# A decoder block's attention stage: the rotary steps on GpSimd one to a slot, filler blocks dealt out evenly, and weight splitting taken off GpSimd behind attention

## The chip, the core and the metric

The kernel runs on one core of one Trainium2 chip, as one program in one launch. The metric is the time of an execution in microseconds (us) on the device; lower is better. A core has five engines with a queue of instructions each: TensorE (PE, matrix products and transposes into PSUM), VectorE (DVE), ScalarE (ACT), GpSimd (POOL) and SyncE (SP, which here only issues DMAs). They run side by side and wait for one another through semaphores. Each takes its own instructions in order, so an instruction that waits holds up everything behind it on its engine.

## What is computed

The reference is one layer of a decoder on 512 tokens of width 1024, in float32:

```python
h = rms_norm(x, norm_mix[l]);  proj = h @ w_in[l]
u, q, kc, vc, ksl, vsl, kwn, vwn, g_nsa, g_merge = jnp.split(proj, IN_SPLITS, axis=-1)
y_pool = pool_mixer(u, w_pool[l], pool_scale[l])
y_nsa = nsa_mixer(q, kc, vc, ksl, vsl, kwn, vwn, g_nsa, ...)
g_a, g_b = jnp.split(sigmoid(g_merge), 2, axis=-1)
merged = g_a * (y_pool @ w_proj_pool[l]) + g_b * (y_nsa @ w_proj_nsa[l])
x = x + merged @ w_out[l]
h = rms_norm(x, norm_mlp[l])
x = x + jnp.square(jax.nn.relu(h @ w_ff1[l])) @ w_ff2[l]
return rms_norm(x, norm_final)
```

`nsa_mixer` is attention with 16 heads of 64 dimensions and two key/value groups, in three branches: over compressed blocks, over selected blocks and over a sliding window. With 512 tokens every block is selected and the window covers everything, so the last two branches are two causal attentions with keys and values of their own. Queries and keys are turned by rotary position tables (`apply_rope`): `y = x*cos + rot(x)*sin`, where `rot` swaps the two halves of a head.

## The kernel before

**Stages.** A first stage projects keys, values, the pooling mixer, the first three query blocks (`q0` to `q2`) and the gates `ga`. The attention stage follows, then the merge with the remaining columns of `w_proj_nsa` (keys `pn2` to `pn7`) and `w_out` (keys `wo`), then the MLP, whose large products are formed from seven smaller ones each (so some sums of weight blocks are made in DRAM beforehand, by DMAs that accumulate).

**Precision.** Each float32 operand is split in a high part `h` and a rest `l`, and a product is three matmuls (h·h, h·l, l·h). Weights arrive by DMA from SP in one of four raw buffers (`emit_load`, line 235), ACT writes `h` (line 351), and the rest is a subtraction (line 353), half a weight block (128x512) at a time. `emit_prep_half` gives the second half's subtraction to GpSimd while `mode["pool"]` is set and to VectorE otherwise. It is set ahead of attention and reset only ahead of the MLP.

**Attention.** A *slot* is one head, one block of 128 queries and one or both of the two causal branches. A pair of heads has 12 slots: four short ones (query blocks 0 and 1, both branches in one slot, `half` 0) and eight long ones (query blocks 2 and 3, one branch a slot, `half` 1, 384 or 512 keys). Eight pairs make 96 slots. The loop at the end of the stage deals with one slot a turn: scores of slot i+1 on PE (line 1014), mask and minimum on DVE (line 1036, `smax`), exponential on ACT (line 1046, `expo`), normalising and gating weights of slot i-1 on GpSimd (line 1059, `weight`), transposes of slot i-4 on PE (line 1076; `LAG` is 4), their split on ACT and DVE (lines 1087 and 1091), and two slots later the products with the values (line 1110). Probabilities have five buffers (`P_BUFS`). Compressed scores of the next pair are a generator of small steps (`cmp_scores`, lines 950 to 986) that `step_side` advances once a slot; three of its steps are on GpSimd (lines 973, 975, 976).

**Fillers.** PE work that does not hang on the slots is put between them: `FILL2` lists 13 blocks, the query blocks `q3` to `q7` and the eight blocks of the other gate (`gb0` to `gb7`), each of 24 matmuls of 128x512 in four pieces of six (`pieces`, line 394, PSUM tile `psF`), followed by the first block of `w_proj_nsa` (`pn0`). `fill()` emits one piece. The loop calls it until `want` is reached, a share that grows evenly with the slots, and once more in each of the first five slots. A query block is followed by its rotary turn, and `fill2` gives back without a piece while a rotary turn of an earlier query block is under way (`while scored["rope"]`).

**Rope.** `rope` (a generator, advanced once a slot) copies the block from PSUM on ACT (`rx`, line 618), lets four DMAs on SP's queue write the swapped halves (`rs`, line 621), multiplies by the cosine table (line 626) and the sine table (line 629) in two halves of 256 columns each, on GpSimd during attention, and adds the two on DVE (line 634). Four multiplications are issued in four consecutive slots, whatever their kind. Then `q_done` splits the block into the `Q` tile (lines 659 to 664).

**Sums in DRAM.** `make_sum` copies a block of `w_ff` to DRAM from SP's queue (line 265), and `add_sum` adds another to it by an accumulating DMA that GpSimd's queue issues (line 273). In the loop, `add_sum(last)` runs in every fourth slot and stands behind that slot's weights.

The order of the instructions on each engine is fixed when the program is built; a scheduler places them by the order of the code and by its own estimate of when they are ready, and `issue_after` (`behind`) ties one instruction to a place behind another.

Of the kernel before, what the change touches and what calls it, by code (L numbers as in the profile page):

```python
# [16 lines left out]
ALU = mybir.AluOpType  # L17
# [45 lines left out]
def trunk(ctx: ExitStack, tc: tile.TileContext, A, out):  # L63
    nc = tc.nc
    PE, ACT, DVE, POOL = nc.tensor, nc.scalar, nc.vector, nc.gpsimd
    PSUM = bass.MemoryType.PSUM

    def pool(name, **kw):
        return tc.tile_pool(name=name, bufs=1, reuse_waits="tile", **kw)
# [35 lines left out]
    def add_key(k):  # L105
        i = int(k[-1]) if k[-1].isdigit() else None
        if k in IN_COLS:
            add_cols(k, w_in, IN_COLS[k])
        elif k[:2] in ("wk", "wv"):
            w = A["w_c" + k[1] + "1"][0]  # L110
            add_w(k, [(w[512 * i:512 * i + 512, :].rearrange("(k p) c -> p k c", p=128), 0)])
        elif k[0] == "V":
            k0, k1 = ((0, 3), (3, 6), (6, 8))[i]
            wv = w_in[k0 * 128:k1 * 128, :].rearrange("(k p) c -> p k c", p=128)
            add_w(k, [(wv[:, :, 1920:2048], 0), (wv[:, :, 2176:2352], 128)])
        elif k == "wpool":
            add_w(k, [(w_pool.rearrange("g c d -> c g d"), 0)])
        elif k[:2] == "pp":
            add_w(k, [(w_pp[:, 256 * i:256 * i + 256].rearrange("(k p) c -> p k c", p=128), 0)])
        else:  # L120
            c0 = {"u": 0, "q": 512, "ga": 2352, "gb": 3376}[k[:-1]]
            add_cols(k, w_in, c0 + 128 * i)
# [1 line left out]
    IN_COLS = {"ck": 1536, "cv": 1664, "ks": 1792, "kw": 2048}  # L124
    P1 = ("ck ks u0 wk0 wk1 u1 wk2 u2 kw wk3 cv V0 V1 V2 wv0 u3 wv1 q0 wv2 wpool ga0 ga1 wv3 ga2 q1 "
          "ga3 ga4 ga5 q2 ga6 ga7 pp0 pp1 pp2 pp3").split()
    FILL2 = "gb0 q3 q4 q5 gb1 gb2 q6 gb3 q7 gb4 gb5 gb6 gb7".split()
    for k in P1 + FILL2:
        add_key(k)
    for j in range(8):  # L130
# [83 lines left out]
    held, begun = {}, deque()  # L214

    def emit_load():
# [20 lines left out]
        if sums_after(i):  # L237
            make_sum(began)
        if i >= len(P1) + len(FILL2) + 4 and (len(begun) > 2 or begun and st["sums"] == len(jobs)):
            add_sum()  # L240
        return True

    def sums_after(i):

        if i < MLP0:
            return len(P1) + 3 <= i < len(P1) + len(FILL2) + 8
        return i % 3 == 0
# [10 lines left out]
    def make_sum(load):  # L258

        if st["sums"] < len(jobs):  # L260
            to, q, _ = jobs[st["sums"]]
            while any(q is jobs[n][0] for n in begun):
                add_sum()
            with tc.issue_after(load.ins):
                nc.sync.dma_start(to, q)
            begun.append(st["sums"])
            st["sums"] += 1

    def add_sum(behind=None):

        to, _, q = jobs[begun.popleft()]
        with tc.issue_after(behind.ins) if behind else nullcontext():
            POOL.dma_start(to, q, accum_op=ALU.add)  # L273

    part = {}
    mode = {"pool": False, "first": POOL}
# [105 lines left out]
    def use(key):  # L382
        i = st["use"]
        st["use"] += 1
        assert WL[i][0] == key, (WL[i][0], key)
        while st["prep"] <= i:
            emit_prep_half()
        return hls.pop(i)
# [21 lines left out]
    def step_side():  # L410
        for _ in range(len(side)):
            g = side.popleft()
            try:
                next(g)
                side.append(g)
            except StopIteration:
                pass

    def drain_side():
        while side:  # L420
            step_side()
# [57 lines left out]
    op = e2.enter_context(pool("op"))  # L479
# [49 lines left out]
    def behind(made):  # L529
        return tc.issue_after(made.ins)  # L530
# [22 lines left out]
    def evac0(i, after=None):  # L553
        sl = slice(128 * i, 128 * i + 128)
        for a in range(2):
            ks = slice(4 * a, 4 * a + 4)
            r = ACT.activation(hT[0][:, ks, sl], trs[i][a], AF.Copy)
            with behind(after) if after else nullcontext():
                v = DVE.tensor_tensor(hT[1][:, ks, sl], trs[i][a], hT[0][:, ks, sl].bitcast(F32), op=ALU.subtract)
        return r, v  # L560
# [9 lines left out]
    r, _ = evac0(1)  # L570
# [32 lines left out]
    cosT, sinT = cst[:, C_COS:C_COS + S], cst[:, C_SIN:C_SIN + S]  # L603
# [4 lines left out]

    scored = {"pairs": 0, "rope": 0}
    last_exp = []  # L610

    def rope(ps, scale, done, after=0):

        assert not scored["rope"]
        scored["rope"] = 1
        xr = ap.tile([128, S], F32, tag="rx", bufs=1, name="rx")
        sw = ap.tile([128, S], F32, tag="rs", bufs=1, name="rs")
        ACT.activation(xr, ps, AF.Copy, scale=scale)
        for b in range(4):
            a = b ^ 1  # L620
            nc.sync.dma_start(sw[32 * b:32 * b + 32, :], xr[32 * a:32 * a + 32, :])
        yield
        eng = POOL if mode["pool"] else DVE
        hs = [slice(0, S // 2), slice(S // 2, S)]
        for c in hs:
            eng.tensor_tensor(xr[:, c], xr[:, c], cosT[:, c], op=ALU.mult)
            yield
        for c in hs:
            eng.tensor_tensor(sw[:, c], sw[:, c], sinT[:, c], op=ALU.mult)
            yield  # L630
        yield
        for c in hs:
            yield
            DVE.tensor_tensor(xr[:, c], xr[:, c], sw[:, c], op=ALU.add)
        while scored["pairs"] < after:
            yield
        for _ in done(xr):
            yield
        scored["rope"] = 0
# [28 lines left out]
    with ExitStack() as c1:  # L668
# [184 lines left out]
        for k in P1[2:]:  # L853
            i = int(k[-1]) if k[-1].isdigit() else None
# [35 lines left out]
    with ExitStack() as c2:  # L890
        p2 = c2.enter_context(pool("p2"))
        ps2 = c2.enter_context(pool("ps2", space=PSUM))
        def fill2():
            for k in FILL2:
                i = int(k[-1])
                if k[0] == "q":
                    while scored["rope"]:
                        yield True
                    post = (lambda i: lambda ps: rope(ps, 1.0, q_done(i), i - 2))(i)
                else:  # L900
                    def post(ps, i=i):
                        ACT.activation(GB[:, i, :], ps, AF.Copy)
                yield from fm(k, ps2, post)
            free.append(True)
            split_ready()
            early[0] = use("pn0") + (ps2.tile([128, S], F32, tag="F", bufs=F_BANKS, name="psF"),)
            for k in range(7):
                while (k, 1) not in split:
                    yield True
                proj_k(early[0], k)  # L910
                if k % 2 or k == 6:
                    ahead()
                    yield
# [20 lines left out]
        fdone = [0]  # L934

        def fill(n=1):
            for _ in range(n):
                if next(filler, True):
                    return False
                fdone[0] += 1  # L940
            return True
# [47 lines left out]
        slots = []  # L989
# [95 lines left out]
        def turn_hi(i):  # L1085
            src, dH, dL = turn_views(i)
            ACT.activation(dH, src, AF.Copy)  # L1087
# [35 lines left out]

        side.append(cmp_scores(0))
        while 0 not in PTc:
            fill()
            step_side()
        n = len(slots)
        total = 4 * len(FILL2) + 4
        done0 = fdone[0]  # L1130
        after = deque()
        score_pe(0)
        for i in range(n + LAG + PLAG):
            if i < n:
                p = slots[i][0]
                if i % 12 == 3 and p + 1 < NPAIR:
                    while p + 1 not in Q:
                        fill()
                        step_side()
                if i % 12 == CMP_AT and p + 1 < NPAIR:  # L1140
                    side.append(cmp_scores(p + 1))
            if i + 1 < n:
                score_pe(i + 1)
                scored["pairs"] = (i + 2) // 12
            t = i - LAG
            if 0 <= t < n:
                turn_pe(t)
                turn_hi(t)
            if i < n:
                smax(i)  # L1150
                expo(i)
            if 0 <= i - 1 < n:
                last = weight(i - 1)
            if i % 4 == 3 and len(begun) > 1:
                add_sum(last)
            if 0 <= t < n:
                turn_lo(t)
            step_side()
            want = done0 + (total - done0) * (i + 1) // (n + LAG + PLAG)
            while fdone[0] < want and fill():  # L1160
                pass
            if i < 5:
                fill()
            j = t - PLAG
            if 0 <= j < n and j % 2 == 1 and pv(j):
                o_evac(*slots[j][0:2])
        for _ in filler:
            pass
        drain_side()
        early[1] = use("pn1") + (ps2.tile([128, S], F32, tag="F", bufs=F_BANKS, name="psF"),)  # L1170
        with tc.issue_after(last_exp[0].ins):
            for j in range(8):
# [93 lines left out]
    with ExitStack() as c3:  # L1266
        q3 = c3.enter_context(pool("q3"))
# [385 lines left out]
```

## Time and profile before

| | us |
|---|---|
| median of 3 runs | 813.62 (812.95 to 814.96) |
| the profiled execution, its own time | 811.65 |
| span of that execution, first to last instruction | 809.8 |
| TensorE busy in it | 788.0 (97%) |
| VectorE busy | 621.4 (77%) |
| ScalarE busy | 491.3 (61%) |
| GpSimd busy | 207.9 (26%) |

The profile is of one execution. Busy times are by engine; a matmul's end is modelled and matmuls overlap, so PE counts as busy also where it is not at its peak, and what tells is its idle time and who ended it. In the views by stretch of time each row gives busy time and number of instructions of each engine, then PEclk, the share of TensorE's clock that was granted, then the mean busy share of the DMA engines and what they moved. In the views of groups, "idle before" is idle time of that engine just ahead of the group, with the work that ended it. Attention lies between about 182 and 390 us of the span.

### The profile page before, as it was taken

The page shows a single profiled execution, that of the slowest core. Times are in us where ns is not written, and L with a number is a line of the kernel's source. Part 1 is how long each engine was busy: PE and PEld are TensorE (multiplying, and loading weights), DVE is VectorE, ACT ScalarE, POOL GpSimd, SP SyncE. Part 2 cuts the span into 40 slices and gives each one's busy share as a digit, 9 for nine tenths or more (in the row PEclk, how much of TensorE's full clock was granted, in tenths as well). Part 3 has the DMA queues.
Part 4 walks back from the last instruction along what each step waited for, and adds up shares of the span by engine and source line. Part 5 has one row for each costly group of instructions (what it writes and reads, how often), then busy time and mean ns, then how long its engine had stood idle before and what let it go on. Part 6 is the DMA issues. An engine that isn't in the chain of part 4 may idle for free.

```text
span 809.8 us, 14149 instructions
## 1 busy us (share of the span) xinstructions
PE 788.0 (97%) x5163; PEld 709.1 (88%) x5163; DVE 621.4 (77%) x1217; ACT 491.3 (61%) x968; POOL 207.9 (26%) x273
## 2 busy tenths in 40 slices
PE   8999999998999999999999999999999999999996
PEld 7889878887788888888788899999999999999996
DVE  5796744547888888888664579996899689978975
ACT  6576533327878788899434476934773477347833
POOL 4000000028777867674334100111111110000000
PEclk9999999999999999999999999999999999999999
DMA  9554632357456524554954807999899997754522
GB/s 306 141 161 120 167 92 92 104 162 164 66 134 136 129 72 93 104 132 93 313 146 155 203 2 217 317 242 284 243 285 225 286 262 207 211 165 156 185 76 105
DMA packets 128752, 136.65 MB, mean 169 GB/s; under 512 B 5349, under 2 KB 117001, under 8 KB 128522
## 3 DMA queue, kind: packets, MB, share of 16 engines
q1 hardware_dynamic: 107274, 113.98, 43.3%
q0 software_dynamic: 21120, 20.97, 18.2%
q8 instruction: 41, 0.67, 0.3%
q10 hardware_dynamic: 288, 0.79, 0.3%
q14 instruction: 29, 0.24, 0.1%
HBM read 131.01 MB, written 44.04 MB: 216 GB/s over the span
## 4 chain that ended last, share of the span: by engine, by line
PE 75%; DVE 14%; ACT 5%; issue 3%; POOL 2%; DMA 1%; SPq 0%; ACTq 0%; DVEq 0%; POOLq 0%
PE psF L394 22%; PE psB L1380 15%; PE psB L394 12%; PE psB L1499 9%; PE psO L1110 3%; PE psT L1076 3%; PE psS L1014 3%; DVE wl L308 2%; PE psV L394 2%; PE psF L451 1%; DVE w3l L308 1%; PE psC L714 1%; DVE P L1036 1%; ACT wh L306 1%; POOL P L1059 1%
## 5 line engine op out<-in xcount | busy, mean ns | idle before, releaser
L394 PE MATMUL psF<-R,wh 128*128 128x512 f32 x512 | 166.6, 404 | 0.8 <-ACT GB L688 0.6
L306 ACT ACTIVATE wh<-raw 128x1024 fp32r<-128x1024 f32 x70 | 74.0, 1058 | 74.0 <-PE psB L1499 32.6
L351 ACT ACTIVATE wh<-raw 128x512 fp32r<-128x512 f32 (+1 forms) x100 | 60.1, 620 | 82.5 <-PE psF L394 38.2
L394 PEld LDWEIGHTS psF<-R,wh 128*128 128x128 f32 x512 | 92.4, 189 | 19.0 <-ACT GB L688 0.9
L273 POOL DMA_DIRECT2D S<-w_ff x40 | 46.4, 1160 | 233.1 <-DMA S<-w_ff 163.5
L394 PE MATMUL psF<-R,wl 128*128 128x512 f32 x256 | 101.9, 398 | 0.4 <-DVE wl L353 0.4
L308 DVE TENSOR_TENSOR wl<-raw,wh 128x1024 fp32r<-128x1024 f32 x70 | 85.3, 1219 | 16.8 <-ACT wh L306 16.7
L1059 POOL TENSOR_SCALAR P<-P,sm,GT 128x128 f32<-128x128 f32 (+3 forms) x128 | 86.0, 708 | 42.2 <-DVE sm L1056 28.7
L353 DVE TENSOR_TENSOR wl<-raw,wh 128x512 fp32r<-128x512 f32 (+1 forms) x74 | 53.5, 734 | 33.3 <-ACT wh L351 32.3
L1046 ACT ACTIVATE P<-P,sm 128x128 f32<-128x128 f32 (+3 forms) x128 | 71.0, 556 | 9.5 <-DVE sm L1036 8.5
L1036 DVE CUSTOM_DVE_ANT_0 P<-psS,cst 128x128 f32<-128x128 f32 (+3 forms) x128 | 59.7, 484 | 6.8 <-PE psT L1076 5.1
L1380 PE MATMUL psB<-R,wh 128*128 128x256 f32 x352 | 64.1, 282 | 0.0
L1087 ACT ACTIVATE PT<-psT 128x512 fp32r<-128x512 f32 (+2 forms) x96 | 49.5, 520 | 19.7 <-PE psT L1076 19.0
L353 POOL TENSOR_TENSOR wl<-raw,wh 128x512 fp32r<-128x512 f32 x28 | 38.1, 1364 | 88.4 <-ACT wh L351 86.1
L306 ACT ACTIVATE w3h<-raw 128x1024 fp32r<-128x1024 f32 x35 | 37.0, 1056 | 39.2 <-PE psB L1499 17.0
L1091 DVE TENSOR_TENSOR PT<-psT,PT 128x512 fp32r<-128x512 f32 (+2 forms) x96 | 56.5, 594 | 3.4 <-ACT PT L1087 2.6
L394 PEld LDWEIGHTS psF<-R,wl 128*128 128x128 f32 x256 | 48.3, 189 | 11.4 <-DVE wl L353 0.6
L1076 PE MATMUL psT<-ident,P 128*128 128x128 f32 x320 | 51.6, 275 | 4.8 <-POOL P L1059 4.0
L1380 PEld LDWEIGHTS psB<-R,wh 128*128 128x128 f32 x352 | 54.1, 189 | 0.3 <-DVE R L1322 0.2
L308 DVE TENSOR_TENSOR w3l<-raw,w3h 128x1024 fp32r<-128x1024 f32 x35 | 42.7, 1220 | 14.4 <-ACT w3h L306 14.4
L1076 PEld LDWEIGHTS psT<-ident,P 128*128 128x128 f32 x320 | 40.0, 142 | 14.7 <-POOL P L1059 6.9
L1380 PE MATMUL psB<-R,wl 128*128 128x256 f32 x176 | 49.5, 281 | 0.0
(385 smaller groups left out, 2295.7 us busy)
## 6 DMA issues: line engine op xcount, KB each, us to landing
raw<-w_ff SPq DMA_DIRECT2D x55, 512.0 KB, 5.2
S<-w_ff POOLq DMA_DIRECT2D x40, 512.0 KB, 7.7
raw<-S SPq DMA_DIRECT2D x40, 512.0 KB, 4.4
raw<-w_in SPq DMA_DIRECT2D x32, 512.0 KB, 3.9
S<-w_ff SPq DMA_DIRECT2D x30, 512.0 KB, 5.4
S<-S SPq DMA_DIRECT2D x10, 512.0 KB, 6.2
raw<-w_proj_nsa SPq DMA_DIRECT2D x8, 512.0 KB, 4.2
raw<-w_out SPq DMA_DIRECT2D x8, 512.0 KB, 3.5
```

The costliest lines, as they stand in the source:

```text
L306: ACT.activation(h, t, AF.Copy)
L308: DVE.tensor_tensor(l, t, h.bitcast(F32), op=ALU.subtract)
L351: ACT.activation(h[:, sl], t[:, sl], AF.Copy)
L353: eng.tensor_tensor(l[:, sl], t[:, sl], h[:, sl].bitcast(F32), op=ALU.subtract)
L394: PE.matmul(ps, a, b, start=first and j == 0, stop=last and j == n - 1, skip_group_check=True)
L1036: DVE.tensor_tensor_reduce(out=P[:, o:o + n].rearrange("p (a c) -> p a c", c=128), in0=s, in1=m, scale=1.0, scalar=3e38, op0=ALU.add, op1= ...
L1046: last_exp[:] = [ACT.activation(c, c, AF.Exp, bias=sm[:, 0, e:e + 1], scale=-1.0, accum_out=sm[:, 1, e:e + 1])]
L1059: r = POOL.tensor_scalar(P[:, o:o + n], P[:, o:o + n], sm[:, 2, e:e + 1], GT[:, qb, c + e:c + e + 1], op0=ALU.mult, op1=ALU.mult)
L1076: PE.transpose(pt[:, 128 * j:128 * j + 128], P[:, 128 * j:128 * j + 128], ident)
L1091: DVE.tensor_tensor(dL, src, dH.bitcast(F32), op=ALU.subtract)
L1380: PE.matmul(out, w[u][:, k, 128 * f:128 * f + 128], XB[x][v][:, k, :], **kw)
L1499: PE.matmul(out, YB[y][u][:, k, 128 * f:128 * f + 128], w[v][:, k, :], **kw)
```

## The change

Four things are changed.

1. **Rope.** The four multiplications are taken in the order cosine and sine of the first half of the columns, then of the second, and on GpSimd each is issued only in a turn of the loop in which `slot["long"]` is set: from the fifth turn on, where the slot whose weights were just issued is a long one. Each is tied to a place behind those weights. The sum of the first half is issued as soon as the second half's cosine step is; the other one turn after the last multiplication.
2. **Fillers.** `FILL2` alternates gate and query blocks (`gb0 q3 gb1 q4 gb2 q5 gb3 q6 q7 gb4 ...`). Ahead of the loop at most eight pieces are emitted, and in a turn at most two; the extra piece in each of the first five turns is gone.
3. **Sums.** `add_sum` starts in turn 11 in place of turn 3.
4. **Weights.** `mode["pool"]` is reset at the end of the loop, so that behind attention VectorE subtracts both halves of a weight block.

```diff
-    FILL2 = "gb0 q3 q4 q5 gb1 gb2 q6 gb3 q7 gb4 gb5 gb6 gb7".split()
+    FILL2 = "gb0 q3 gb1 q4 gb2 q5 gb3 q6 q7 gb4 gb5 gb6 gb7".split()
...
+    slot = {"long": False, "scaled": None}
...
         hs = [slice(0, S // 2), slice(S // 2, S)]
         for c in hs:
-            eng.tensor_tensor(xr[:, c], xr[:, c], cosT[:, c], op=ALU.mult)
-            yield
-        for c in hs:
-            eng.tensor_tensor(sw[:, c], sw[:, c], sinT[:, c], op=ALU.mult)
-            yield
+            for t, table in ((xr, cosT), (sw, sinT)):
+                while mode["pool"] and not slot["long"]:
+                    yield
+                with behind(slot["scaled"]) if mode["pool"] else nullcontext():
+                    eng.tensor_tensor(t[:, c], t[:, c], table[:, c], op=ALU.mult)
+                yield
+                if c is hs[1] and t is xr:
+                    DVE.tensor_tensor(xr[:, hs[0]], xr[:, hs[0]], sw[:, hs[0]], op=ALU.add)
         yield
-        for c in hs:
-            yield
-            DVE.tensor_tensor(xr[:, c], xr[:, c], sw[:, c], op=ALU.add)
+        DVE.tensor_tensor(xr[:, hs[1]], xr[:, hs[1]], sw[:, hs[1]], op=ALU.add)
...
         while 0 not in PTc:
-            fill()
+            if fdone[0] < 8:
+                fill()
             step_side()
...
                 last = weight(i - 1)
-            if i % 4 == 3 and len(begun) > 1:
+                slot.update(long=i > 3 and slots[i - 1][1] == 1, scaled=last)
+            if i > 7 and i % 4 == 3 and len(begun) > 1:
                 add_sum(last)
...
             want = done0 + (total - done0) * (i + 1) // (n + LAG + PLAG)
-            while fdone[0] < want and fill():
-                pass
-            if i < 5:
-                fill()
+            for _ in range(2):
+                if fdone[0] < want:
+                    fill()
...
         drain_side()
+        mode["pool"] = False
         early[1] = use("pn1") + (ps2.tile([128, S], F32, tag="F", bufs=F_BANKS, name="psF"),)
```

## The prediction

> **What bounds the kernel now.** I read the page first, then busy time by stretch, then who made TensorE (PE) wait, then the chain of waits and the timeline where it waits most. Engines busy:
>
> ```profile
> PE 788.0 (97%) x5163; PEld 709.1 (88%) x5163; DVE 621.4 (77%) x1217; ACT 491.3 (61%) x968; POOL 207.9 (26%) x273
> ```
>
> PE sets the end, and since the change leaves its matmuls as they are, time can only come from what PE loses: idle time and a lower clock. The stretches of attention and of the stage behind it (columns: length, then PE, PEld, DVE, ACT, POOL busy, granted clock, DMA):
>
> ```profile
> 182.10:200.10 18.00, 15.21 (x85) 12.38 (x84) 13.79 (x53) 12.15 (x38) 14.25 (x20) 0.91 0.74 169
> 200.10:223.40 23.30, 21.35 (x144) 18.10 (x142) 20.01 (x66) 19.91 (x55) 16.95 (x25) 1.00 0.46 70
> 223.40:238.50 15.10, 14.53 (x79) 12.02 (x79) 12.42 (x39) 11.50 (x31) 10.19 (x15) 1.00 0.36 103
> 238.50:271.30 32.80, 32.61 (x214) 28.82 (x213) 29.00 (x100) 26.42 (x72) 24.58 (x34) 1.00 0.75 154
> 271.30:302.90 31.60, 30.53 (x198) 26.77 (x198) 28.39 (x89) 26.14 (x69) 22.66 (x33) 1.00 0.38 93
> 382.00:393.00 11.00, 9.33 (x47) 7.57 (x46) 6.42 (x10) 7.92 (x15) 2.61 (x2) 1.00 1.13 286
> 393.00:487.00 94.00, 93.82 (x468) 78.19 (x466) 59.37 (x82) 44.26 (x83) 22.66 (x17) 1.00 0.54 154
> ```
>
> Length less PE busy: idle 2.79, 1.95, 0.57, 0.19, 1.07, 1.67 and 0.18 us. The first two rows are pairs 0 and 1 of heads, and they hold more than half. The merge behind attention leaves PE no idle time to win. Who ended the waits inside attention:
>
> ```profile
> PE psT L1076 <- POOL P L1059: 4.0, 3, 2.2
> PE psB L394 <- ACT mH L1280: 1.7, 1, 1.7
> PE psT L1076 <- ACT pc L986: 0.7, 1, 0.7
> PE psT L984 <- DVE PT L1091: 0.6, 1, 0.6
> PE psF L394 <- DVE wl L353: 0.4, 1, 0.4
> ```
>
> The largest is the transposes' wait for weighted probabilities. Two of the three, in pair 0, and the chain ahead of them, in order of time (start, length, work):
>
> ```profile
> 192.93 0.44 PE L1076 MATMUL psT<-ident,P 128*128 128x128 f32 x2 [2.21 <-POOL P L1059]
> 193.94 0.44 PE L1076 MATMUL psT<-ident,P 128*128 128x128 f32 x2 [0.58 <-POOL P L1059]
> ```
>
> ```profile
> 185.51 1.93 POOL P L1059 x5
> 188.33 1.21 POOL S L273
> 189.53 1.47 POOL rx L626 x2
> 191.00 1.35 POOL rs L629 x2
> 192.35 1.55 POOL P L1059 x2
> ```
>
> GpSimd issues an accumulating DMA (1.21 us) and four rope steps (1.47 + 1.35) in one piece, and the next weights stand behind them. What follows is dearer still, since PE ran at a lower clock afterwards:
>
> ```profile
> 190.70:194.85 4.15, 1.36 (x9) 1.03 (x8) 3.14 (x7) 0.76 (x3) 4.15 (x7) 1.00 0.78 121
> 194.85:198.27 3.42, 3.42 (x12) 2.61 (x11) 2.02 (x9) 1.96 (x6) 2.56 (x4) 0.54 0.52 158
> ```
>
> Over 3.42 us the grant was 0.54. What PE did there would take 3.42 x 0.54 = 1.85 us at full speed: 1.6 us lost on top.
>
> A sentence apart: the Trainium skill (TensorE: Matmul & The Clock Gate, "What's actually happening") has the clock halve after an idle window of about 3.4 us; here PE was still busy for 1.36 of the 4.15 us ahead of the drop, so the trace has it at less than a whole idle window, and I follow the trace: the drop goes when the stall goes. By the rule read strictly the stall didn't cause it, and the sum below would be 1.6 us smaller.
>
> **The change, part by part.**
>
> *Startup stall (rope and first sum).* In the built order of the changed kernel the first accumulating DMA stands ahead of GpSimd's first attention work, and behind it come eight weights without a break, then weight and rope step by turns. The DMA's source:
>
> ```profile
> 161.59 0.61 SPq L265 DMA_DIRECT2D S<-w_ff  x1
> S<-w_ff SPq DMA_DIRECT2D x2, 512.0 KB, 4.9
> 171.19 1.36 POOL L353 TENSOR_TENSOR wl<-raw,wh 128x512 fp32r<-128x512 f32 x1 [43.90 <-ACT wh L351]
> ```
>
> Issued at 161.59 with 4.9 us to land, it is there by about 166.5, and GpSimd idles until 171.19: the moved DMA costs nothing. SP's copy of its result, which precedes weight loads in SP's queue, also starts sooner. Against the 2.79 us idle and 1.6 us of clock (4.4 together) I take 4.0, bounds 1.5 to 4.4, since the first slots fill a pipeline and some waiting may only surface elsewhere.
>
> *The second rope.* In pair 1 the wait for weights is 4.0 less the 2.21 and 0.58 of pair 0 = 1.2 us, again behind a block of rope steps. I take 1.2, bounds 0 to 1.8 (with the 0.6 of L984).
>
> *Spreading itself.* What a long slot now asks of GpSimd while a rope turn is under way (group, busy, mean ns, idle before):
>
> ```profile
> L1059 POOL TENSOR_SCALAR P<-P,sm,GT 128x512 f32<-128x512 f32 x32 | 27.4, 857 | 16.7 <-DVE sm L1056 11.9 <-PE psT L1076 2.0 <-DVE c L971 1.5
> L1059 POOL TENSOR_SCALAR P<-P,sm,GT 128x384 f32<-128x384 f32 x32 | 24.8, 802 | 13.6 <-DVE sm L1056 11.3 <-PE psT L1076 1.6 <-PE psS L1014 0.3
> L273 POOL DMA_DIRECT2D S<-w_ff x16 | 18.6, 1165 | 4.2 <-DMA raw<-S 4.2
> L629 POOL TENSOR_TENSOR rs<-rs,cst 128x256 f32<-128x256 f32 x10 | 8.9, 937 | 0.0
> L626 POOL TENSOR_TENSOR rx<-rx,cst 128x256 f32<-128x256 f32 x10 | 8.0, 911 | 0.0
> L353 POOL TENSOR_TENSOR wl<-raw,wh 128x512 fp32r<-128x512 f32 x13 | 17.3, 1329 | 16.6 <-ACT wh L351 16.6
> L976 POOL TENSOR_TENSOR PC<-cw,PC 128x256 fp32r<-128x256 f32 x7 | 5.2, 736 | 0.4
> ```
>
> Four such slots: weights 4 x 0.83, steps 4 x 0.92, one accumulating DMA 1.17, and the compressed scores' three steps, bounded above by 3 x 0.74 = 2.2: 10.4 us, 11.7 with a weight half (1.33). That is above the four slots' 8.3 us (row below). The transposes trail by four slots, which covers 2 to 3.5 us once, and then eight slots without rope pay it back (4 x 0.83 of work each four). Cost between 0 and 3.4 us a rope, five ropes; I take 0.1 each, 0.5, because of this row, where a whole rope turn ran and PE did not idle. Weights now also hold the rope back; in the built order its result stands two slots ahead of its first use at the tightest place (`q6`, slot 63). Sums dropped from turns 3 and 7 are needed in the MLP alone, and by the end of attention the built orders have issued as many.
>
> *Fillers.* The price of a filler from four slots of the same kind (16 to 19 and 28 to 31), few fillers against many; the second pair of rows counts the filler matmuls alone:
>
> ```profile
> 208.30:215.00 6.70, 6.66 (x49) 5.93 (x49) 6.54 (x28) 6.40 (x22) 5.74 (x10) 1.00 0.56 106
> 238.50:246.80 8.30, 8.30 (x57) 7.43 (x56) 7.58 (x26) 5.46 (x16) 6.79 (x9) 1.00 1.09 290
> 208.30:215.00 6.70, 0.88 (x2) 1.00 0.56 106
> 238.50:246.80 8.30, 3.27 (x12) 1.00 1.09 290
> ```
>
> Ten fillers fewer save 1.60 us, 0.16 each; where PE is the bound six take 1.40 us:
>
> ```profile
> 244.02 1.39 PE psF L394 x6
> ```
>
> That is 0.233 each, so a filler that is missing here and made up later costs 0.07 us (in the starved row DVE is busy 6.54 of 6.70). In the built orders, slots 0 to 23 hold 33 fillers before and 60 after, which wins 27 x 0.07 = 1.9 us. But `q7` stands right behind `q6` and has to wait for its rope: slots 44 to 47 and 52 to 59 get 4 fillers where there were 30 and slots 48 to 51 get 24, so about 20 to 30 are late: 1.4 to 2.1 us lost. Net I take +0.2 won, bounds -2.5 to +1.9 (won). The 0.4 us wait for a weight half (L353) is in 223 to 238, where the fillers crowd (39 in slots 24 to 27); even shares end it: 0.4, bounds 0 to 0.6. The fourth rope turn's stretch (271 to 303, idle 1.07) had rope in short slots: I take 0.5, bounds 0 to 1.07.
>
> *No weights on GpSimd behind attention.* Thirteen halves move to DVE (groups of 392 to 520 us; the last row is a line's spread, min/median/max ns):
>
> ```profile
> L353 POOL TENSOR_TENSOR wl<-raw,wh 128x512 fp32r<-128x512 f32 x9 | 13.1, 1460 | 25.0 <-ACT wh L351 22.7 <-issue 2.3
> L353 POOL TENSOR_TENSOR W1L<-raw,W1H 128x512 fp32r<-128x512 f32 x4 | 6.0, 1516 | 0.0
> L888 DVE TENSOR_TENSOR GB<-GB,MA x8: 679/1784/2609, 390.2 to 430.5; 128x512 f32<-128x512 f32 x8
> ```
>
> On DVE such a pass takes 0.68 at its least (L888), 13 x 0.68 = 8.8 us, and DVE's busy time of 393 to 487 would rise from 59.4 to 68.2 of 94, less what L888 regains from its 1784 ns. PE hides it; without that cover it would cost up to 8.8. One place gains: PE's 1.67 us at 391 waits for merges on DVE that ran beside GpSimd's subtraction. A half more now stands ahead of the second merge (0.68), against 1.1 us that L888 gives back: I take 0.4, bounds -0.7 to 1.1.
>
> Sum: 4.0 + 1.2 + 0.2 + 0.4 + 0.5 + 0.4 - 0.5 = 6.2 us won; I take off 0.8 for waits that only move, nearly all the idle time of 182 to 303 that the list of waits doesn't name (6.57 less 4.0, 0.7, 0.6 and 0.4 is 0.9), so 5.4. The profiled execution took 811.65 us, 1.85 beyond its span: 806.2. It lies 1.97 below the median of the runs, so the forecast for that is 813.62 - 5.4 = 808.2.
>
> **The rivals.** *Everything goes, nothing comes* (17%): 4.4 + 1.8 + 0.6 + 1.07 + 1.1, half of the fillers' 1.9, less the 0.8: 9.1 us, 804.5. For it: pairs 2 to 7 show that PE can run without idling. *The startup wait is only half rope's* (13%): weights may wait for ACT and DVE at the start; 808.2 + 2.5 = 810.7. *The stall moves* (15%): `q6` and `q7` starve PE in slots 52 to 59 as pair 0 does now, with the clock's drop, at 4.4: 812.6. Against it: that starved row has PE idle for 0.04 us. *GpSimd becomes the bound* (8%, slower): from the point at which its backlog in a rope turn passes the four slots' lag, weights are late by 2.1 to 3.4 us in each of five turns, 2.8 on average: 14 against 6.7 won, 820.9. Against it: 6.79 us busy of 8.30 in the row with a whole rope turn. *The clock drop stays* (5%): it has a cause other than this stall, and the 1.6 remains: 809.8. By the Trainium skill's strict reading (that page and section) this would hold. That the change doesn't do what it says is out: the built order shows the alternation.
>
> **How the numbers follow.** Forecast 808.2 with 42%. The low end takes in the full win, 804.0; the high end reaches past the moved stall to 814.0, leaving out the GpSimd bound and the tails. About 0.3% (2.4 us) is what a measurement of this kernel tells from none. Faster than 811.2: the forecast, the full win, nearly all of half rope's and of the kept drop, 0.72; the moved stall and edges 0.17; slower 0.11, with some room for what I haven't seen.
>
> **What would show it.** Right: no wait of transposes for L1061 over 0.5 us in pairs 0 and 1, a clock of 1.00 from 185 to 390, PE idle in 182 to 223 under 1.5 us, the wait ahead of the merge near 1.3, and an MLP as long as before (322.8 us from 487). Wrong: a second clock drop near slots 52 to 60, GpSimd busy without a break for over 10 us with PE waiting for it, or PE waiting for L353 on DVE behind attention.

## The result and the profile after

The changed kernel is slower: a median of 817.61 us (816.81 to 818.48, 6 runs) beside 813.59 (812.59 to 815.04, 6 runs) for the kernel before, a ratio of 1.0049 with an interval of 1.0034 to 1.0063, or 4.0 us. Forecast was 808.2. One of the executions timed for the experiments below (e5) took 2714 us and is left out of every figure. The profiled execution took 818.32 (span 816.5, before 809.8), so 2.7 of the 6.7 us between the two spans are particular to the two executions that were profiled.

Busy time by engine on the page of the changed kernel:

```profile
PE 789.3 (97%) x5163; PEld 711.1 (87%) x5163; DVE 620.9 (76%) x1231; ACT 491.4 (60%) x968; POOL 188.4 (23%) x259
```

The work is the same. Stretches of the changed kernel (columns as before): the turns of attention, all of attention, and the MLP; and all of attention in the kernel before.

```profile
182.00:200.00 18.00, 17.14 (x106) 14.64 (x105) 16.09 (x59) 15.30 (x45) 14.15 (x22) 1.00 0.44 132
200.00:223.70 23.70, 23.10 (x148) 20.08 (x147) 20.35 (x69) 19.30 (x54) 15.69 (x22) 1.00 0.60 124
223.70:237.60 13.90, 10.04 (x56) 8.38 (x55) 8.62 (x29) 8.14 (x23) 11.24 (x18) 0.88 0.68 113
237.60:320.40 82.80, 80.16 (x518) 70.02 (x517) 71.85 (x238) 66.80 (x178) 55.25 (x79) 1.00 0.47 98
320.40:333.40 13.00, 8.63 (x53) 6.89 (x52) 9.82 (x24) 8.16 (x19) 10.44 (x14) 0.98 0.63 136
333.40:397.50 64.10, 63.65 (x395) 55.74 (x394) 51.38 (x163) 55.60 (x143) 35.13 (x46) 0.98 0.48 109
...
182.30:397.46 215.16, 202.38 (x1264) 175.48 (x1262) 178.07 (x580) 173.31 (x458) 141.90 (x196) 0.98 0.51 110
...
493.60:816.50 322.90, 313.08 (x2540) 307.47 (x2540) 271.44 (x336) 183.37 (x260) 24.82 (x21) 1.00 0.77 217
```

```profile
182.05:390.42 208.37, 201.30 (x1263) 173.87 (x1262) 176.57 (x580) 172.83 (x458) 143.62 (x198) 0.99 0.53 116
```

Attention is 6.8 us longer: PE's idle time rises from 208.37 - 201.30 = 7.1 to 12.8 us, and its busy time, in which a lower clock shows, by 1.1. The start is as wanted: idle falls from 2.79 and 1.95 us to 0.86 and 0.60, at a clock of 1.00. But two short stretches that were quiet before now have 3.9 and 4.4 us of idle time. The MLP is unchanged. Who ended PE's waits within attention and just behind it, in the changed kernel (total, times, longest; the four largest):

```profile
PE psT L1078 <- DVE PT L1093: 5.2, 5, 3.0
PE psO L1103 <- DVE oT L1121: 4.0, 5, 1.3
PE psT L986 <- DVE PT L1093: 2.9, 1, 2.9
PE psB L394 <- DVE GB L889: 1.2, 1, 1.2
```

GpSimd's weights, which led this list before with 4.0 us, are gone from it. All four entries name DVE. What DVE itself waited for at the rotary additions (L634 and L636), in the changed kernel and then in the one before:

```profile
DVE rx L634 <- POOL rs L631: 6.6, 3, 3.5
DVE rx L636 <- POOL rs L631: 2.2, 2, 1.3
```

```profile
DVE rx L634 <- POOL rs L629: 1.5, 1, 1.5
```

The chain of waits of the changed kernel through the second of these places (start, length, work) shows how GpSimd's lateness gets to PE:

```profile
215.43 3.62 issue
...
219.08 1.07 POOL wl L353
...
220.37 0.76 POOL P L1061
...
221.81 1.22 POOL P L1061
223.03 0.70 POOL rx L631
...
228.20 0.75 POOL P L1061
228.95 0.62 POOL S L273
...
229.63 1.21 POOL rs L631
...
230.86 0.98 DVE rx L636
...
232.42 0.85 ACT PT L1089 x2
233.27 0.56 DVE PT L1093
...
233.97 0.72 PE psT L986 x4
```

GpSimd's timeline at the head of the two places, in the changed kernel, with the idle time before and what ended it; then DVE's at the additions:

```profile
219.08 1.29 POOL L353 TENSOR_TENSOR wl<-raw,wh 128x512 fp32r<-128x512 f32 x1 [3.66 <-ACT wh L351]
...
320.49 0.73 POOL L631 TENSOR_TENSOR rx<-rx,cst 128x256 f32<-128x256 f32 x1 [2.98 <-DMA rs<-rx]
```

```profile
225.65 0.62 DVE L634 TENSOR_TENSOR rx<-rx,rs 128x256 f32<-128x256 f32 x1 [2.81 <-POOL rs L631]
...
230.86 0.98 DVE L636 TENSOR_TENSOR rx<-rx,rs 128x256 f32<-128x256 f32 x1 [1.34 <-POOL rs L631]
...
322.60 0.82 DVE L634 TENSOR_TENSOR rx<-rx,rs 128x256 f32<-128x256 f32 x1 [3.48 <-POOL rs L631]
...
328.93 1.47 DVE L636 TENSOR_TENSOR rx<-rx,rs 128x256 f32<-128x256 f32 x1 [0.90 <-POOL rs L631]
```

GpSimd stands for 3.66 us (second rope turn) until ACT has split a weight block, and for 2.98 us (fifth) until the rotary copies land. What has piled up then runs in one piece, from 219.08 to beyond 230: a weight half, weights, two accumulating DMAs, the compressed scores' three steps, and the four rope steps that now stand singly behind weights. DVE has reached the addition long before and stands, 4.15 us in the second turn and 4.38 in the fifth. Behind the addition in DVE's queue are masks and the splits of transposes (`PT`), and PE waits for those. In the built order the additions stand only two slots or so behind the step that they need: the rope steps of the second turn are in slots 21 to 24 (counted from 1, as for the additions below; the prediction counts slots from 0) and the additions in 24 and 26; before, the steps were in 16 and 17 and the additions in 21 and 22.

Each of PE's two long gaps is followed by a stretch at half the clock, as the one gap of the kernel before was (windows that hold the gap, and those behind it):

```profile
230.55:233.97 3.42, 0.51 (x4) 0.10 (x2) 2.88 (x9) 2.09 (x7) 2.39 (x4) 1.00 1.02 131
233.97:237.38 3.41, 3.41 (x15) 3.22 (x16) 1.93 (x8) 2.85 (x8) 1.86 (x4) 0.50 0.14 22
329.54:332.95 3.41, 1.26 (x8) 1.14 (x9) 3.37 (x10) 1.84 (x5) 1.24 (x2) 1.00 0.58 143
332.95:336.36 3.41, 3.41 (x16) 3.21 (x15) 3.04 (x11) 3.15 (x10) 1.82 (x2) 0.50 0.57 191
```

A grant of 0.50 over 3.41 us costs 1.7 us, twice where it was once.

### The profile page after: what moved, and what is told of

It is laid out like the page before. It is cut to its first block, busy times and chain, and to the rows that moved or that the text cites. A ratio compares the mean times of both kernels' runs of the same rounds, so it can differ in the third digit from the quotient of the medians.

```text
span 816.5 us, 14128 instructions
## 1 busy us (share of the span) xinstructions
PE 789.3 (97%) x5163; PEld 711.1 (87%) x5163; DVE 620.9 (76%) x1231; ACT 491.4 (60%) x968; POOL 188.4 (23%) x259
## 4 chain that ended last, share of the span: by engine, by line
PE 70%; DVE 15%; ACT 7%; issue 3%; POOL 3%; DMA 1%; SPq 0%; ACTq 0%; POOLq 0%; DVEq 0%
PE psF L394 21%; PE psB L1384 14%; PE psB L394 12%; PE psB L1503 9%; PE psO L1112 3%; PE psS L1016 2%; PE psT L1078 2%; DVE wl L308 2%; PE psV L394 2%; ACT P L1048 1%; PE psF L451 1%; DVE P L1038 1%; POOL P L1061 1%; DVE w3l L308 1%; DVE PT L1093 1%
## 5 line engine op out<-in xcount | busy, mean ns | idle before, releaser
L1061 POOL TENSOR_SCALAR P<-P,sm,GT 128x128 f32<-128x128 f32 (+3 forms) x128 | 86.7, 711 | 45.3 <-DVE sm L1058 31.6
L353 DVE TENSOR_TENSOR wl<-raw,wh 128x512 fp32r<-128x512 f32 (+1 forms) x84 | 59.0, 714 | 34.9 <-ACT wh L351 34.5
L1112 PE MATMUL psO<-PT,VV 128*128 128x256 f32 x320 | 48.4, 290 | 0.0
```

What stands on the lines that cost most here:

```text
L1061: r = POOL.tensor_scalar(P[:, o:o + n], P[:, o:o + n], sm[:, 2, e:e + 1], GT[:, qb, c + e:c + e + 1], op0=ALU.mult, op1=ALU.mult)
L1112: PE.matmul(ps[:, qb % 2, :, :], VV[:, k, b, g, :], t[:, j, :, :], start=False, stop=last and j == len(kbs) - 1 and t is tL, skip_group_ch ...
```

## The experiments

The leading theory after the comparison: the loss is the place of the two additions in DVE's queue. The rivals: the spread steps themselves (GpSimd's backlog), the fillers' new order, DVE's additional weight halves, and, as sources of the backlog, the weight halves and the accumulating DMAs on GpSimd. Ratios are to the kernel before, run on the same chip.

**The additions later (e1, e11).** The rest of the change is kept; both additions are issued behind the last step and tied behind the loop's latest mask on DVE, three slots behind that step (slots 12, 27, 48, 61 and 72).

```diff
-                if c is hs[1] and t is xr:
+                if c is hs[1] and t is xr and eng is DVE:
                     DVE.tensor_tensor(xr[:, hs[0]], xr[:, hs[0]], sw[:, hs[0]], op=ALU.add)
         yield
-        DVE.tensor_tensor(xr[:, hs[1]], xr[:, hs[1]], sw[:, hs[1]], op=ALU.add)
+        for c in hs if eng is POOL else hs[1:]:
+            with behind(slot["smax"]) if eng is POOL else nullcontext():
+                DVE.tensor_tensor(xr[:, c], xr[:, c], sw[:, c], op=ALU.add)
...
-                DVE.tensor_tensor_reduce(
+                slot["smax"] = DVE.tensor_tensor_reduce(
```

> The changed kernel, with rope's two additions on VectorE put behind the mask and minimum of the third slot after the last GpSimd step (they stood two slots behind their steps in the second and the fifth rope turn); nothing else moves. Theory A (VectorE, which takes its instructions in order, stands at the addition while GpSimd is late: 8.8 us waited for rope's sine steps, two PE stalls of 3.1 us with a clock drop each): those waits go below 1.5 us, both clock drops go, 808 to 811 us. Theory B (GpSimd's backlog makes the weights themselves late, the addition only shows it): the transposes then wait for weights, PE idles as long, 816 to 818 us.

Measured: 809.08 us (808.55 to 809.42, 4 runs) against 813.38, ratio 0.9941 (0.9921 to 0.996); span 807.0. Its stretches, DVE's one wait for the rope, and PE's longest waits:

```profile
182.00:200.00 18.00, 17.64 (x109) 15.03 (x108) 15.70 (x59) 16.29 (x47) 15.22 (x23) 1.00 0.43 131
200.00:223.70 23.70, 22.75 (x146) 19.71 (x145) 20.83 (x70) 18.66 (x52) 14.23 (x21) 1.00 0.63 127
223.70:237.60 13.90, 13.84 (x93) 12.00 (x92) 12.13 (x38) 11.06 (x31) 12.48 (x18) 1.00 0.61 108
...
320.40:333.40 13.00, 11.79 (x77) 10.10 (x76) 11.68 (x40) 11.16 (x33) 8.78 (x14) 1.00 0.56 122
```

```profile
DVE rx L640 <- POOL rs L631: 0.8, 1, 0.8
```

```profile
PE psO L1107 <- DVE oT L1125: 2.5, 5, 1.3
PE psB L394 <- DVE GB L893: 1.2, 1, 1.2
PE psT L990 <- DVE PT L1097: 1.2, 1, 1.2
```

Idle time at the two places falls from 3.9 and 4.4 us to 0.06 and 1.2, and no stretch of attention has a lower clock. So the place of two additions, with GpSimd's steps where the change puts them, is worth the difference of the ratios, 0.0108 or 8.8 us. GpSimd's unbroken run is still there (12.48 us busy of 13.90); it just isn't waited for. e11 is the same kernel on another chip, for the size of its gain:

> The changed kernel with late additions once more, timed in five rounds beside the kernel before on this chip: 808 to 810 us where the kernel before takes 812 to 814, a ratio of 0.993 to 0.996.

809.72 (808.68 to 810.03, 5 runs) against 812.52, ratio 0.9964 (0.995 to 0.9978). Faster than the kernel before here too, by a little less than expected; by this ratio the additions' place is worth 0.0085 or 6.9 us.

**The rope in a block, as before (e2).** Before's two multiplication loops and additions, in the changed kernel.

```diff
-            for t, table in ((xr, cosT), (sw, sinT)):
...
+            eng.tensor_tensor(xr[:, c], xr[:, c], cosT[:, c], op=ALU.mult)
+            yield
+        for c in hs:
+            eng.tensor_tensor(sw[:, c], sw[:, c], sinT[:, c], op=ALU.mult)
+            yield
```

> The changed kernel with rope as before (four steps in consecutive slots, additions as before), fillers, sums and weights as changed. Theory A and B both put the loss into rope's spreading: 808 to 811 us. Theory C (the new order of fillers, with q7 behind q6, costs the time): 815 us or more, with PE idle in slots 44 to 63.

811.75 (810.39 to 813.54, 10 runs), ratio 0.9977 (0.9965 to 0.9989). DVE still waited, since among the new fillers the additions again come close behind the steps (slots 24 and 26 in the second turn):

```profile
DVE rx L635 <- POOL rs L630: 5.7, 3, 3.7
```

That made PE gaps of 2.5 us at the most, and no drop of the clock. The block is better than the spread steps with close additions, and by the medians worse than either with late ones (e1, e7; its interval just overlaps e7's). That no drop came is of this one profiled execution: the ten of e2 had mean clocks of 0.992 to 0.998.

**The block with late additions (e7).** As e2, with both additions tied as in e1.

```diff
+        for c in hs:
+            yield
+            with behind(slot["smax"]) if eng is POOL else nullcontext():
+                DVE.tensor_tensor(xr[:, c], xr[:, c], sw[:, c], op=ALU.add)
```

> Rope's four GpSimd steps as before (consecutive turns, any slot), both additions four to five slots behind the last step; fillers, sums and weights as changed. If spreading the steps is worth what the prediction gave it (2 us or more at the second and later turns): 811 us or more. If only the place of the additions counts: 808 to 810 us, as with the steps spread.

809.08 (808.93 to 809.4, 6 runs) against 812.01, ratio 0.9956 (0.9942 to 0.9971), the same as e1 within the intervals. So once the additions are late, spreading the steps has no effect that these runs can tell.

**The fillers as before (e3).** `FILL2`, the calls ahead of the loop and those in it as before.

```diff
-    FILL2 = "gb0 q3 gb1 q4 gb2 q5 gb3 q6 q7 gb4 gb5 gb6 gb7".split()
+    FILL2 = "gb0 q3 q4 q5 gb1 gb2 q6 gb3 q7 gb4 gb5 gb6 gb7".split()
...
-            for _ in range(2):
-                if fdone[0] < want:
-                    fill()
+            while fdone[0] < want and fill():
+                pass
+            if i < 5:
+                fill()
```

> The changed kernel with the fillers as before (order, number ahead of the loop and in its turns), rope, sums and weights as changed. Theory C: back to 811 to 814 us. Theory A: rope's additions still stand one to two slots behind their steps, so a stall of VectorE of 2 us or more stays in some rope turn: 815 us or more.

815.34 (812.97 to 819.28, 10 runs), ratio 1.0027 (1.0009 to 1.0045). Still slower than before, with DVE waiting 6.7 us for the rope, and PE again waiting for late weights in the second turn (3.2 us). The fillers are not the cause.

**Weights on GpSimd behind attention, as before (e4).** One line is taken back.

```diff
-        mode["pool"] = False
```

> The changed kernel with weights on GpSimd behind attention as before. All theories: the merge has no idle PE either way, so 817.6 us within 1 us; 0.4 us slower by the prediction's term for it.

818.16 (817.88 to 819.38, 4 runs), ratio 1.0055 (1.0037 to 1.0073). PE's wait ahead of the merge is again 1.7 us and not 1.2; the total does not separate from that of the change.

**No weight halves on GpSimd at all in attention (e5, e9).**

```diff
-            eng = POOL if mode["first"] or part["half"] and mode["pool"] else DVE
+            eng = POOL if mode["first"] else DVE
```

> The changed kernel, with both halves of a filler's weight subtraction on VectorE during attention too; rope's steps and additions as changed. Theory D (GpSimd gets late in the second rope turn because a weight subtraction at the head of its queue stood 3.7 us waiting for ScalarE's copy, to 219.0, with attention's weights and rope's steps behind it): VectorE's wait for rope in the second turn falls from 4.2 us to under 1 us and the clock drop at 234 goes; the fifth turn's wait (4.4 us, where GpSimd waited for rope's own copies by DMA) stays; 811 to 814 us. Theory E (the accumulating DMAs that GpSimd issues inside rope turns make it late): the waits stay, 816 us or more.

812.84 (811.41 to 814.66, 9 runs) against 812.01, ratio 1.0004 (0.999 to 1.0017): most of the loss comes back. e9 is the same kernel, with the profile that is read here:

> The kernel without weight subtractions on GpSimd during attention once more, for a profile of an undisturbed execution. Theory D: VectorE waits under 1 us for rope's sine steps in the second turn (4.2 us in the changed kernel), GpSimd reaches those steps without having stood for a subtraction, and the drop of the clock near 234 us is gone; a wait of 3 to 4.4 us stays in the fifth turn. If the second turn's wait stays at 2 us or more, the time that this kernel won has another source.

813.69 against 812.52 (one run). In the second turn DVE's waits fall from 4.15 to 1.36 + 0.49 = 1.85 us, not to under 1, and the drop of the clock there is gone; the fifth turn keeps its 3.19 + 0.90 and its drop. And the picture behind the expectation falls. GpSimd's timeline at the same place:

```profile
218.72 0.77 POOL L1061 TENSOR_SCALAR P<-P,sm,GT 128x512 f32<-128x512 f32 x1 [3.74 <-ACT wh L351]
```

GpSimd stands as long with no subtraction to do (3.74 us, was 3.66). The profile names ACT here too, but these weights also need DVE's reciprocal (`sm`), which ran from 218.37 to 218.53, and their exponential was done by 216.93; which of the two engines held them isn't shown. What is saved for certain is the subtraction's own 1.3 us in the backlog.

**No accumulating DMA during a rope (e6).**

```diff
-            if i > 7 and i % 4 == 3 and len(begun) > 1:
+            if i > 7 and i % 4 == 3 and len(begun) > 1 and not scored["rope"]:
```

> The changed kernel, with no accumulating DMA issued by GpSimd while a rope turn is under way (they move behind it; one is left in the fifth turn). Theory E: 811 to 814 us, VectorE's wait for rope in the second turn under 1 us. Theory D: that wait stays over 2 us, 816 us or more.

815.44 (814.21 to 816.2, 10 runs) against 812.01, ratio 1.0034 (1.0022 to 1.0046). The first additions wait as long as in the change (2.84 and 3.51 us); only the second turn's second falls, from 1.34 to 0.17, and with it that turn's drop of the clock, which is missing from e4's profile too, with DVE waiting there as in the change. A small part.

**Late additions and no weight halves on GpSimd (e8).** The edits of e1 and e5 together.

> The late additions of the first experiment together with no weight subtraction on GpSimd. If with late additions GpSimd's lateness reaches nobody (theory A): 809.1 us within 1.5 us, or a little slower for the 13 passes more on VectorE. If late weights still cost PE something: 806 to 807 us.

808.86 (807.59 to 810.4, 6 runs) against 812.01, ratio 0.9951 (0.9935 to 0.9967). No better than e1 by what the intervals tell: with late additions, relieving GpSimd adds nothing measurable.

**Late additions in the kernel before (e10).** The additions there are tied to the latest mask in the same way; from the third turn on they come 3 to 5 slots later.

> The kernel before, with its additions of the third, fourth and fifth rope turn three to five slots later than they stood (the first two stay where they are); all else as before. There VectorE waited 1.5 us for rope in all, at the first turn, and the startup stall is GpSimd's block of work, so theory A leaves nothing to win here: the same as before within 1.5 us. If it gains 3 us or more, the place of the additions was a cost of the kernel before as well, and the changed fillers, sums and order of GpSimd's work are not what makes the late-additions version faster.

812.02 (810.25 to 814.0, 10 runs) against 812.52, ratio 0.9991 (0.998 to 1.0002): no difference. Its longest wait of PE is the one that the change takes away:

```profile
PE psT L1080 <- POOL P L1063: 4.0, 3, 2.2
```

So late additions alone win nothing, and the change alone loses; the two together (e1, e11) win 0.4 to 0.6%, the best version run here, with e7 and e8 level with it.

## Why the prediction was wrong

**Startup stall and second rope: right.** Forecast 4.0 + 1.2. In the changed kernel idle time of 182 to 223.7 us is 1.46 and was 4.74, and the drop of the clock at 195 is gone: 3.3 + 1.7 = 5.0 us. No transposes wait for L1061, and the rival that only half of the startup wait is rope's falls.

**The clock drop goes with the stall: right**, and the rival that it stays falls. The grant was 0.50 and not 0.54 (the prediction's row starts 0.25 us ahead of the drop), so the drop cost 1.7 us and not 1.6. The new gaps brought new drops, which the sum had not foreseen since it foresaw no gaps.

**No weights on GpSimd behind attention: right.** Forecast 0.4; the wait ahead of the merge went from 1.7 to 1.2 us, and the MLP from 322.8 to 322.9.

**The fourth turn (rope in short slots): the size came, the mechanism is not shown.** With late additions 271 to 303 us has PE idle for 0.37 us, by this row of e1, and 1.07 before: 0.7 against 0.5. But in the kernel before, the four steps on GpSimd of that turn already stood among weights of long slots (277.28 to 281.99), and PE's wait of 0.7 us there named ACT's `pc`.

```profile
271.00:303.00 32.00, 31.63 (x209) 27.48 (x208) 29.43 (x98) 27.25 (x72) 20.40 (x30) 1.00 0.40 91
```

The same row is against the rival that the stall moves to `q6` and `q7`, whose slots 52 to 59 lie there.

**Fillers, +0.2 (bounds -2.5 to 1.9): not settled within the bounds**, of which the lower is below what the prediction's own terms give (1.9 won less 2.1 lost). e3 and the change differ by 0.0022 in the ratio, 1.8 us in favour of the old order, with intervals that overlap and with a wait for late weights back in the second turn. The wait for a weight half (L353), 0.4, is gone as forecast; with the old order it is there (0.6). What the new order is worth beside late additions was not tried.

**Spreading itself, -0.5: this step failed.** It weighed GpSimd's work of four slots (10.4 to 11.7 us) against their 8.3 and let the four slots' lag of the transposes cover the excess. The backlog came as worked out, in two of five turns. What failed is the consumer: it asked when weights are late for PE's transposes, and of the rope's result only that "in the built order its result stands two slots ahead of its first use". That first use is in slot 63, where the next pair's scores need the finished `Q`. Ahead of it stands the addition on DVE, two slots behind GpSimd's step, and DVE takes its queue in order: from then on all of DVE's work for the slots waited with it. The lag covers transposes from late weights, not masks and `PT` splits from a standing DVE. Price, in the profiled execution: 3.9 + 4.4 us of idle time and twice 1.7 of clock, 11.7, where 0.5 stood; the medians have 8.8 by e1 and 6.9 by e11. The row that would have shown it was in the profile of before (DVE waiting 1.5 us at L634), and both built orders had the additions' places, 24 and 26 where the steps end in 24.

**The rival "GpSimd becomes the bound" (820.9)** had the right engine and the right sign, and its sign to look for (GpSimd busy without a break for over 10 us) came; but PE waited for DVE, in two turns, not for weights in five. Late additions with the same backlog are faster than before, so the backlog is not the bound.

**Waits that only move, -0.8: too small by e11.** With the additions late the change wins 2.8 (e11) to 4.3 us (e1) of the forecast 5.4; e11's interval ends at 4.1 us, e1's at 6.4. The profile of e1 has new idle time between 237.6 and 271, 0.34 + 1.30 + 0.64 = 2.3 us by these rows, where 238.5 to 271.3 had 0.19 before and 237.6 to 270.7 had 0.52 in the changed kernel:

```profile
237.60:250.00 12.40, 12.06 (x77) 10.20 (x76) 10.84 (x36) 9.94 (x27) 10.17 (x14) 1.00 0.92 170
250.00:260.00 10.00, 8.70 (x60) 7.62 (x60) 8.23 (x33) 8.45 (x27) 4.82 (x9) 1.00 0.49 133
260.00:271.00 11.00, 10.36 (x69) 9.14 (x69) 10.38 (x33) 8.48 (x21) 10.19 (x16) 1.00 0.37 50
```

Which edit makes these waits was not tried.

## What to carry to other kernels

When an operation is spread or delayed on a slack engine, look up where its consumer stands in the consumer's own queue, and price a late result by everything behind that consumer, not by the final use of the result. A consumer with slots to spare before its result is needed can be placed late, in the kernel before at no cost that the runs can tell (e10), and here that placement decided the sign of the whole change. An engine that was hardly waited for (PE waited 1.7 us for DVE in the attention of before) becomes a bound when one of its instructions is placed close behind a late result.

## What the hardware showed that was not expected

The clock fell after gaps shorter than the stretch over which it stayed low: after idle times of 2.91 and 3.01 us in the changed kernel, and after 2.4 us in e7, for 3.4 us each time; in e2 a gap of 2.5 us brought no drop. Nor did the gap of 2.91 us (230.92 to 233.83) in e4, whose attention is built as the changed kernel's is. What differs is the gap's place. The two drops of the changed kernel start 98.98 us apart, 29.0 times 3.413 us. On a grid of that step, laid through each trace's own drops, all nine drops that fall inside the program in these traces (e5's aside) follow a stretch in which PE was busy for 1.6 us or less, and no stretch with 1.68 us or more brought one. The two nearest cases are the kernel before, with a drop, and then e4 without, where the grid cuts the gap in two:

```profile
191.69:195.10 3.41, 1.59 (x9) 1.06 (x9) 3.33 (x8) 0.60 (x1) 3.41 (x5) 1.00 0.73 115
195.10:198.51 3.41, 3.41 (x12) 2.82 (x12) 2.07 (x7) 1.79 (x5) 2.55 (x4) 0.50 0.61 163
```

```profile
232.10:235.51 3.41, 1.68 (x14) 1.67 (x15) 3.15 (x12) 3.34 (x10) 1.81 (x3) 1.00 0.73 116
235.51:238.92 3.41, 3.41 (x25) 3.07 (x24) 2.69 (x10) 3.41 (x12) 3.06 (x5) 1.00 0.00 0
```

The Trainium skill (TensorE: Matmul & The Clock Gate, "What's actually happening") has the halving follow an idle window of about 3.4 us. By these traces a window that is idle for a little over half suffices (ends of matmuls are modelled, so the limit is an estimate). The page also calls that window free-running, and the traces agree: the same gap lay inside one window in the changed kernel and across two in e4. So whether the gap in the second rope turn costs 1.7 us of clock is luck of timing, and the number of drops seems to change between executions: the changed kernel's six had mean clocks of 0.993 to 0.997, and a drop takes 0.002 of the mean.

A subtraction of two SBUF operands on DVE, with a median of 0.69 us, took 4.28 us once (e7), while GpSimd ran without a break from 316.03 to 319.74; PE waited 2.4 us behind it. The mask operation, which reads one operand from PSUM, kept its 0.68 to 0.69 us (mean of 32) in the kernel before, the changed one and e1.

```profile
316.03 4.28 DVE L353 TENSOR_TENSOR wl<-raw,wh 128x512 fp32r<-128x512 f32 x1 [0.36 <-ACT wh L351]
```

The Trainium skill (SBUF — State Buffer, "Who interferes with whom") says that a DVE instruction with two SBUF inputs contends with a GpSimd instruction that reads SBUF; this row agrees, though no run here isolates it.

The rotary copies ahead of the fifth turn took 5.7 us at the median to land in the changed kernel, where that of all five turns is 2.4; what slowed them was not tried.
